# Summing weight blocks in the transfer: four operand sums of a Strassen-type down product move from VectorE to accumulating transfers

## The chip, the cores and the metric

One core of one Trainium2 chip. The time is that of one execution on the device in microseconds (us). The kernel before takes 1230.37 us (median of 3 runs, 1229.37 to 1232.88); its profiled execution took 1231.72 us, of which the trace spans 1229.9. Engines: PE is TensorE, PEld its weight loads, DVE is VectorE, ACT is ScalarE, POOL is GpSimd, SP is SyncE, which issues all transfers of the kernel before. Lnnn is a line of the kernel; most additions, subtractions and products of two tiles stand under one helper's line (L894 `tt`, L138 `sub`), so tiles tell them apart.

## The reference, cut to what matters

One layer of a decoder on 1024 tokens of width 1024, float32. Its last part is the gated MLP:

```python
h = rmsnorm(x, ffn_pre_norm)
u = causal_depthwise_conv(h @ w_up, conv_w, conv_b)     # 1024 x 5632
gate, up = split(u, 2)
y = (gelu(gate) * up) @ w_down                          # 1024 x 2816 @ 2816 x 1024
x = x + rmsnorm(y, ffn_post_norm)                       # y * rsqrt(mean(y*y) + eps) * g
```

The change touches `@ w_down`, the norm and the sum behind it, that is, the last 235 us.

## The kernel before, in words

**The down product.** Tokens, the 2816 inner rows and the 1024 output columns are each halved, and the product of the two 2x2 block matrices is formed from seven block products instead of eight (the Winograd form of Strassen's method). They run in the order P1, P2, P7, P5, P6, P3, P4 (`PASS`). Each is 512 tokens by 1408 by 512: 11 *pairs* `p` (ND = 11) of 128 inner rows, and in each pair four token tiles of 128 (`down`). Operands are split into a rounded part and a rest (`split`: ACT casts, L923; DVE subtracts, L138), and three matmuls of 512 columns (L141 to L143, `mm3`) replace one. A pair is so 12 matmuls, a product 132.

**Weights.** P1, P2 and P3 use a block of the weights as it is: w1 and w2 are the upper and lower 1408 rows, LO and HI the halves of the columns. Four products need sums of blocks:

```
P7: w2[HI] - w1[HI]           P5: w1[HI] - w1[LO], stored to td[0]
P6: w2[HI] - td[0], stored to td[1]        P4: w2[LO] - td[1]
```

`w_load` brings both terms into one 128x1024 tile `dwr` by SP's queue, `t_sum` subtracts on DVE (L894 `dwr<-dwr`), SP stores what a later product needs. `td` lies in DRAM. The tiles have a tag of their own with six buffers (PB), so a load waits until the tile six before it is done with.

**Activations.** The left operands `dg` are loaded from DRAM once; `s_sum` builds S1 to S4 in place on DVE (L894 `dg<-dg`).

**Results.** `evac` takes each product's four PSUM tiles to the SBUF tiles `y`, `combine` adds the products up, `norm1` takes the squares (ACT, L119, into `junk`, sums in `dsq`) and multiplies `y` by the norm's gains `gff` in place (DVE); it so waits for ACT to have read `y`. `norm2` adds up the two sums of squares (L1256), forms mean + eps (L111), takes the power -1/2 on POOL (L112) and does y * r + x on DVE (L1260, two halves), and SP stores the rows.

**The tail.** The last three pairs (TAIL) of P4 are not run pair by pair but token tile by token tile: all three pairs of tile 4, then of tile 5, 6 and 7, so that tile 4 can go through `evac`, `norm1` and `norm2` while PE works on tile 5.

**What sets the order.** Each step is put in a list with a time in units of one pair (`at_`; `t0` is the pair's own time, `tf_` the same with the last pairs moved together). The list is sorted and issued in this order, and ACT, DVE, POOL and PE keep it (`manual_schedule`). The times only order; they make nothing wait. SP's transfers are not in it: a scheduler puts them in order by when it thinks them ready, and SP issues them strictly one after another, each when its own waits are over.

Of the kernel before, what the change touches and what calls it, by code (L numbers as in the profile page):

```python
# [9 lines left out]
F32 = mybir.dt.float32  # L10
# [49 lines left out]
def trunk_kernel(ctx: ExitStack, tc: tile.TileContext, a: dict, out: bass.AP):  # L60
# [832 lines left out]
    def tt(eng, out_, x, y, op):  # L893
        eng.tensor_tensor(out=out_, in0=x, in1=y, op=op)  # L894
# [262 lines left out]
                "P6": lambda: g1[p][:, LO], "P3": lambda: g2[p][:, LO], "P4": lambda: g2[p][:, HI]}[m]()  # L1157

    def b_of(m, p):
        return wr[m, p][:, HI if m == "P5" else LO]  # L1160

    def w_load(m, p):
        early = m == "P1"
        t = wr[m, p] = S("dwr", tag="s" if early else "p", bufs=None if early else PB)
        w1, w2 = a["w_down"][p], a["w_down"][ND + p]
        src = {"P1": ((LO, w1[:, LO]),), "P2": ((LO, w2[:, LO]),), "P7": ((LO, w1[:, HI]), (HI, w2[:, HI])),
               "P5": ((slice(0, 1024), w1),), "P6": ((LO, w2[:, HI]), (HI, td[0, p])), "P3": ((LO, w2[:, HI]),),
               "P4": ((LO, w2[:, LO]), (HI, td[1, p]))}[m]
        for sl, x in src:
            load(t[:, sl], x)  # L1170

    def t_sum(m, p):
        t = wr[m, p]
        if m == "P7":
            tt(V, t[:, LO], t[:, HI], t[:, LO], ALU.subtract)
        elif m == "P5":
            tt(V, t[:, HI], t[:, HI], t[:, LO], ALU.subtract)
            load(td[0, p], t[:, HI])
        else:
            tt(V, t[:, LO], t[:, LO], t[:, HI], ALU.subtract)  # L1180
            if m == "P6":
                load(td[1, p], t[:, LO])

    def s_sum(m, p):
        a1, a2 = g1[p], g2.get(p)
# [10 lines left out]
    def form(m, p, side):  # L1196
        forms[m, p, side] = split(b_of(m, p) if side else a_of(m, p))
        if side:
            del wr[m, p]
        elif m == "P4":  # L1200
            del g2[p]

# [43 lines left out]
    def norm1(t, c):  # L1246
        if t not in sqs:
            sqs[t] = cst.tile([P, 2], F32, name=f"dsq{t}")
        hs = blk(c, 512)
        square_sum(sqs[t][:, c:c + 1], y[t][:, hs])  # L1250
        tt(V, y[t][:, hs], y[t][:, hs], env2["g"][:, hs], ALU.mult)

    def norm2(t):
        xt = env2.pop(("x", t))
        s_, r = sm("zs", 1), sm("zr", 1)
        V.tensor_reduce(out=s_, in_=sqs[t], axis=AX.X, op=ALU.add)  # L1256
        rstd(r, s_, D)
        for c in range(2):
            hs = blk(c, 512)
            V.scalar_tensor_tensor(out=y[t][:, hs], in0=y[t][:, hs], scalar=r, in1=xt[:, hs], op0=ALU.mult, op1=ALU.add)  # L1260
            if t == NT - 1:
                load(out[0, blk(t), hs], y[t][:, hs])
        if t < NT - 1:
            load(out[0, blk(t), :], y[t])

    def x_get(t):
        env2["x", t] = S("x2r", tag="pt", bufs=2) if t < 2 else S("x2r")
        load(env2["x", t], x2d[blk(t), :])

    TAIL = 3  # L1270
    down_items = []

    def at_(tm, f, *x):
# [142 lines left out]
```

## Time and profile before

| | |
|---|---|
| median of 3 runs | 1230.37 us |
| profiled execution, and its span | 1231.72 us, 1229.9 us |
| PE, DVE, ACT, POOL busy in the span | 94%, 75%, 47%, 23% |
| chain of work that ended last | PE 72%, DVE 13%, DMA 6%, issue 3% |
| down product: first and last matmul | 995.4 us, 1214.38 us |
| last matmul to the end of the span | 15.5 us |

The shares are means over stages of quite different kinds; the down product and its norm are the stage from 995.4 us to the end. The seven products begin at 995.4, 1025.35, 1055.27, 1085.19, 1115.11, 1146.53 and 1176.70 us. Four of them take 29.92 us to a hundredth or three, which is 132 matmuls without a gap, 0.2267 us each, and 2.72 us for a pair. That makes the unit of the time list 2.72 us.

### The profile page before, as it was taken

Reading aid. Unit: us, or ns where it says so; the run is one execution under the profiler, and the core shown is the slowest. Engines: PE = TensorE matmul, PEld = TensorE weight load, DVE = VectorE, ACT = ScalarE, POOL = GpSimd, SP = SyncE. Lnnn points to the kernel's source line nnn. Section 1 sums busy time; section 2 is a strip of 40 time slices with the busy share of each in tenths; the row PEclk is TensorE's granted clock in tenths of the full one; section 3 lists DMA queues with packets and bytes.
Section 4 is the critical chain, followed back from the end, with each engine's and each line's share of the span. In section 5 each row is a group of like instructions: output and inputs, shape, how many; then the busy total and the mean of one; then the engine's idle time right before and its main releaser. Section 6 shows DMA issues by size and latency. Waiting matters only on the chain.

```text
span 1229.9 us, 15584 instructions
## 1 busy us (share of the span) xinstructions
PE 1154.8 (94%) x5634; PEld 957.8 (78%) x5634; DVE 917.1 (75%) x1393; ACT 581.5 (47%) x1175; POOL 284.3 (23%) x186
## 2 busy tenths in 40 slices
PE   7987989899987899999999999999999999999993
PEld 6965877678875688877888888888888888887872
DVE  6225664745568988864578998898898988896996
ACT  6313552224356677754554544443444455354441
POOL 1132231315259445450001122122121210000000
PEclk9997998889998999999999999999999999999997
DMA  9373222612293123123022221221212289577673
GB/s 344 117 238 104 70 59 79 224 35 69 70 252 73 35 69 87 54 92 113 18 86 94 79 103 69 86 94 61 103 69 86 103 314 353 161 224 232 196 240 137
DMA packets 68461, 156.47 MB, mean 127 GB/s; under 512 B 7168, under 2 KB 23088, under 8 KB 68384
## 3 DMA queue, kind: packets, MB, share of 16 engines
q1 hardware_dynamic: 68384, 155.48, 38.2%
q8 instruction: 44, 0.72, 0.2%
q14 instruction: 33, 0.27, 0.1%
HBM read 116.78 MB, written 37.63 MB: 126 GB/s over the span
## 4 chain that ended last, share of the span: by engine, by line
PE 72%; DVE 13%; DMA 6%; issue 3%; ACT 3%; POOL 1%; SPq 1%; DVEq 0%; POOLq 0%; ACTq 0%
PE p L141 6%; PE p L143 6%; PE p L142 6%; PE scd L608 3%; PE xz L141 3%; PE xz L142 3%; DVE wf L138 3%; PE xz L143 3%; PE psct L141 2%; PE psct L143 2%; PE psct L142 2%; PE accd L641 2%; PE pso L143 2%; PE pso L141 2%; PE pso L142 2%
## 5 line engine op out<-in xcount | busy, mean ns | idle before, releaser
L871 DVE SCALAR_TENSOR_TENSOR u<-C,cw,u 128x1023 f32<-128x1023 f32 (+1 forms) x88 | 112.3, 1278 | 11.5 <-ACT u L868 11.4
L894 POOL TENSOR_TENSOR sq<-sq,sq 128x512 f32<-128x512 f32 x18 | 29.5, 1638 | 354.2 <-DVE sq L894 354.2
L868 ACT ACTIVATE u<-C,cw 128x1024 f32<-128x1024 f32 x44 | 54.8, 1245 | 113.4 <-DVE C L894 88.3
L923 ACT CAST wf<-dwr 128x512 fp32r<-128x512 f32 x77 | 48.0, 623 | 83.1 <-DVE dwr L894 66.1
L141 PE MATMUL p<-h2h,wf 128*128 128x512 f32 x216 | 84.0, 389 | 0.0
L142 PE MATMUL p<-h2l,wf 128*128 128x512 f32 x216 | 84.0, 389 | 0.0
L143 PE MATMUL p<-h2h,wf 128*128 128x512 f32 x216 | 84.0, 389 | 0.0
L138 POOL TENSOR_TENSOR wl<-wraw,wh 128x1024 fp32r<-128x1024 f32 (+1 forms) x25 | 54.5, 2181 | 109.8 <-DVE wh L132 52.7
L112 POOL TENSOR_TENSOR zr<-var,mhalf 128x1 f32<-128x1 f32 x24 | 13.2, 549 | 262.2 <-DVE var L111 262.2
L141 PE MATMUL psct<-hTh,wh 128*128 128x512 f32 x176 | 71.4, 406 | 1.9 <-DVE oBC L588 1.5
L641 PE MATMUL accd<-pt,v 128*128 128x256 f32 (+1 forms) x336 | 60.5, 300 | 11.7 <-ACT pt L134 5.3
L134 ACT CAST pt<-tpd 128x512 fp32r<-128x512 f32 (+1 forms) x80 | 42.1, 543 | 60.2 <-PE tpd L631 48.4
L142 PE MATMUL psct<-hTl,wh 128*128 128x512 f32 x176 | 70.1, 398 | 0.0
L143 PE MATMUL psct<-hTh,wl 128*128 128x512 f32 x176 | 70.0, 397 | 0.0
L618 ACT ACTIVATE pd<-scd,nm 128x128 f32<-128x128 f32 (+3 forms) x64 | 47.5, 744 | 42.9 <-DVE nm L616 28.3
L641 PEld LDWEIGHTS accd<-pt,v 128*128 128x128 f32 x336 | 50.5, 200 | 19.1 <-ACT pt L134 7.9
L138 DVE TENSOR_TENSOR wf<-wraw,wf 128x512 fp32r<-128x512 f32 x90 | 61.5, 683 | 2.7 <-ACT wf L923 2.7
L138 DVE TENSOR_TENSOR pt<-tpd,pt 128x512 fp32r<-128x512 f32 (+1 forms) x80 | 49.5, 632 | 17.5 <-ACT pt L134 17.2
L138 DVE TENSOR_TENSOR wf<-dwr,wf 128x512 fp32r<-128x512 f32 x77 | 52.6, 684 | 12.1 <-ACT wf L923 11.9
L141 PE MATMUL xz<-hTf,wf 128*128 128x512 f32 x144 | 56.0, 389 | 0.0
L143 PE MATMUL p<-hTf,wf 128*128 128x512 f32 x144 | 56.0, 389 | 0.0
L143 PE MATMUL xz<-hTf,wf 128*128 128x512 f32 x144 | 56.0, 389 | 0.0
(291 smaller groups left out, 3561.3 us busy)
## 6 DMA issues: line engine op xcount, KB each, us to landing
wraw<-in_w_up_dram SPq DMA_DIRECT2D x44, 512.0 KB, 4.2
dwr<-in_w_down_dram SPq DMA_DIRECT2D x77, 256.0 KB, 4.9
gd<-u SPq DMA_DIRECT2D x22, 512.0 KB, 2.6
dg<-gd SPq DMA_DIRECT2D x22, 512.0 KB
wraw<-in_wqk_dram SPq DMA_DIRECT2D x11, 512.0 KB, 4.3
dwr<-in_w_down_dram SPq DMA_DIRECT2D x11, 512.0 KB, 5.0
td<-dwr SPq DMA_DIRECT2D x22, 256.0 KB, 5.3
dwr<-td SPq DMA_DIRECT2D x22, 256.0 KB, 4.3
```

Of the source, the lines that this page charges most:

```text
L134: A.copy(dst, src)
L138: (eng or G).tensor_tensor(out=dst, in0=x, in1=hi.bitcast(F32), op=ALU.subtract)
L141: T.matmul(ps, lhsT=lh, rhs=rh, start=start, stop=False)
L142: T.matmul(ps, lhsT=lh, rhs=rl, start=False, stop=False)
L143: T.matmul(ps, lhsT=ll, rhs=rh, start=False, stop=stop)
L608: T.matmul(sc[:, off + c0:off + c1], lhsT=ql[0:rows, blk(i)], rhs=kl[0:rows, c0:c1], start=x == 0, stop=x == len(passes) - 1)
L618: A.activation(p[:, 0:n], s, AF.Exp, bias=nm, accum_out=den[:, i, hd["d"]:hd["d"] + 1])
L641: T.matmul(acc[:, cs], lhsT=hd["v"][:, j], rhs=pt[:, x, bs], start=j == 0 and x == 0, stop=d == 1 and x == 1 and (o == len(ops) - 1 or (o ...
L868: A.activation(us[i], ct2[i], AF.Identity, bias=cw[:, i, 3:4], scale=cw[:, i, 2:3])
L871: V.scalar_tensor_tensor(out=us[i][:, d:], in0=ct2[i][:, 0:SEQ - d], scalar=cw[:, i, 2 - d:3 - d], in1=us[i][:, d:], op0=ALU.mult, op1=ALU ...
L894: eng.tensor_tensor(out=out_, in0=x, in1=y, op=op)
L923: A.copy(f[:, 0], x)
```

## The change

The four sums over weight blocks are made by transfers that add what they read in DRAM to what lies in SBUF (`accum_op=ALU.add`, issued by POOL, `w_add`). The first term is loaded by SP as before and, where it has a minus sign, negated in place on ACT (`w_neg`). The chain of signs is turned so that every second term is added: P7 is -w1[HI] + w2[HI], stored to td[0]; P5 is -w1[LO] + w1[HI], no longer stored; P6 is td[0] + w1[LO]; after P6 has been split it is negated on ACT and stored to td[1] (`w_keep`); P4 is td[1] + w2[LO]. A weight tile now holds two pairs. Loads come 7.6 pairs ahead instead of 4.6, negations 6.0, additions 5.6; the splits stay where they were, at 2.2 and 1.8.

S4 is formed before P6 instead of behind it. The product with the gains goes to a new tile `yg`, and `norm2` is cut in two: `norm_r` (sum, mean, power) and, later in the list, the two halves of y * r + x. TAIL is 4.

```diff
     def b_of(m, p):
-        return wr[m, p][:, HI if m == "P5" else LO]
+        return wr[m, p // 2][:, blk(p % 2, 512)]
 
     def w_load(m, p):
-        early = m == "P1"
-        t = wr[m, p] = S("dwr", tag="s" if early else "p", bufs=None if early else PB)
+        if (m, p // 2) not in wr:
+            early = m == "P1"
+            wr[m, p // 2] = S("dwr", tag="s" if early else "p", bufs=None if early else PB)
         w1, w2 = a["w_down"][p], a["w_down"][ND + p]
...
+        load(b_of(m, p), {"P1": w1[:, LO], "P2": w2[:, LO], "P7": w1[:, HI], "P5": w1[:, LO], "P6": td[0, p],
+                          "P3": w2[:, HI], "P4": td[1, p]}[m])
+
+    def w_neg(m, p):
+        A.mul(b_of(m, p), b_of(m, p), -1.0)
+
+    def w_add(m, p):
+        w1, w2 = a["w_down"][p], a["w_down"][ND + p]
+        G.dma_start(out=b_of(m, p), in_={"P7": w2[:, HI], "P5": w1[:, HI], "P6": w1[:, LO], "P4": w2[:, LO]}[m],
+                    accum_op=ALU.add)
         if m == "P7":
-            tt(V, t[:, LO], t[:, HI], t[:, LO], ALU.subtract)
-        elif m == "P5":
-            tt(V, t[:, HI], t[:, HI], t[:, LO], ALU.subtract)
-            load(td[0, p], t[:, HI])
-        else:
-            tt(V, t[:, LO], t[:, LO], t[:, HI], ALU.subtract)
-            if m == "P6":
-                load(td[1, p], t[:, LO])
+            load(td[0, p], b_of(m, p))
+
+    def w_keep(p):
+        w_neg("P6", p)
+        load(td[1, p], b_of("P6", p))
...
         if side:
-            del wr[m, p]
+            if m == "P6":
+                w_keep(p)
+            if p % 2 or p == ND - 1:
+                del wr[m, p // 2]
...
         square_sum(sqs[t][:, c:c + 1], y[t][:, hs])
-        tt(V, y[t][:, hs], y[t][:, hs], env2["g"][:, hs], ALU.mult)
+        tt(V, y[t, 2][:, hs], y[t][:, hs], env2["g"][:, hs], ALU.mult)
...
-    TAIL = 3
+    TAIL = 4
...
-            at_(tf_ - (5.5 if m == "P1" else 4.6), w_load, m, p)
+            at_(tf_ - (5.5 if m == "P1" else 4.6 if m in ("P2", "P3") else 7.6), w_load, m, p)
+            if m in ("P7", "P5"):
+                at_(tf_ - 6.0, w_neg, m, p)
             if m not in ("P1", "P2", "P3"):
-                at_(tf_ - 2.7, t_sum, m, p)
+                at_(tf_ - 5.6, w_add, m, p)
...
             elif m == "P6":
-                at_(t0 + 5.2, s_sum, "S4", p)
+                at_(t0 - 1.2, s_sum, "S4", p)
...
                 at_(e0 + 0.06, norm1, t + 4, 0)
-                at_(e0 + 0.07, norm2, t + 4)
+                at_(e0 + 0.3, norm_r, t + 4)
+                at_(e0 + 0.6 if t == 3 else e0 + 1.12, norm2, t + 4)
...
-        at_(e6 + 2.2 + 1.6 * t, norm2, t)
+        at_(e6 + 2.2 + 1.6 * t, norm_r, t)
+        at_(e6 + 2.9 + 1.6 * t, norm2, t)
```

**DVE at the end of P4.** `dt` and `dm` are the PSUM tiles of P4, `gff` the gains, `x2r` the residual rows. Before, token tiles 4 and 5:

```order
L894 TENSOR_TENSOR y_9623<-dt_10432,y_9623 128x512
L894 TENSOR_TENSOR y_9623<-y_9623,gff_9889 128x512
L1256 TENSOR_REDUCE zs_10687<-dsq4_10256 128x1
L111 TENSOR_SCALAR var_10690<-zs_10687 128x1
L1260 SCALAR_TENSOR_TENSOR y_9623<-y_9623,zr_10688,x2r_10563 128x512 x2
L894 TENSOR_TENSOR y_9633<-dm_10440,y_9633 128x512
L894 TENSOR_TENSOR y_9633<-y_9633,gff_9889 128x512
```

The same place of the changed kernel:

```order
L894 TENSOR_TENSOR y_9628<-dt_10424,y_9628 128x512
L894 TENSOR_TENSOR yg_10246<-y_9628,gff_9883 128x512
L1260 TENSOR_REDUCE zs_10652<-dsq4_10245 128x1
L111 TENSOR_SCALAR var_10655<-zs_10652 128x1
L894 TENSOR_TENSOR y_9636<-dm_10434,y_9636 128x512
L894 TENSOR_TENSOR yg_10297<-y_9636,gff_9883 128x512
L1268 SCALAR_TENSOR_TENSOR yg_10246<-yg_10246,dr4_10653,x2r_10537 128x512 x2
L1260 TENSOR_REDUCE zs_10679<-dsq5_10296 128x1
```

The evacuation and the gains of tile 5 now stand between the mean of tile 4 and the two instructions that need tile 4's power from POOL.

**ACT while P7 runs.** Casts of P7's operands (`dg` activations, `dwr` weights). Before:

```order
L923 CAST wf_9442<-dwr_9376 128x512
L923 CAST wf_9459<-dg_8858 128x512
L923 CAST wf_9465<-dwr_9403 128x512
L923 CAST wf_9482<-dg_8886 128x512
L923 CAST wf_9488<-dwr_9426 128x512
```

In the changed kernel, for pairs 5 to 8 of P7; `dwr_9455` and `dwr_9501` are P5's tiles for pairs 0, 1 and 2, 3:

```order
L923 CAST wf_9464<-dg_8855 128x512
L1171 ACTIVATE dwr_9431<-dwr_9431 128x512
L923 CAST wf_9471<-dwr_9329 128x512
L923 CAST wf_9487<-dg_8883 128x512
L1171 ACTIVATE dwr_9455<-dwr_9455 128x512
L923 CAST wf_9494<-dwr_9329 128x512
L923 CAST wf_9510<-dg_8905 128x512
L1171 ACTIVATE dwr_9455<-dwr_9455 128x512
L923 CAST wf_9517<-dwr_9380 128x512
L923 CAST wf_9532<-dg_8927 128x512
L1171 ACTIVATE dwr_9501<-dwr_9501 128x512
```

A negation of a later pair's weights now stands between the two casts of each pair.

**SP around the start of P5's loads.** `td` is the sum's place in DRAM. Before, P5's tiles `dwr_9607` to `dwr_9709` hold one pair each:

```order
L97 DMA dwr_9607<-in_w_down_dram 128x1024
L97 DMA dwr_9635<-in_w_down_dram 128x1024
L97 DMA td_5934<-dwr_9518 128x512
L97 DMA td_5934<-dwr_9540 128x512
L97 DMA dwr_9663<-in_w_down_dram 128x1024
L97 DMA dwr_9686<-in_w_down_dram 128x1024
L97 DMA td_5934<-dwr_9562 128x512
```

Now, where `dwr_9280` to `dwr_9431` are P7's tiles from pair 4 on, and `dwr_9455` to `dwr_9546` P5's:

```order
L97 DMA td_5934<-dwr_9280 128x512
L97 DMA dwr_9455<-in_w_down_dram 128x512 x2
L97 DMA td_5934<-dwr_9280 128x512
L97 DMA td_5934<-dwr_9329 128x512 x2
L97 DMA td_5934<-dwr_9380 128x512 x2
L97 DMA dwr_9501<-in_w_down_dram 128x512 x2
L97 DMA td_5934<-dwr_9431 128x512
L97 DMA dwr_9546<-in_w_down_dram 128x512 x2
```

A store of a sum now stands ahead of loads for P5, and it waits for the accumulating transfer that makes the sum. On POOL the 44 accumulating transfers follow the last addition of the up stage with nothing between them, and the eight powers stand behind all of them.

## Rows read from the trace of the kernel before

**Rows 1.** windows, by product: us; busy PE, PEld, DVE, ACT, POOL; clock, DMA share, GB/s

```profile
995.40:1025.35 29.95, 29.89 (x133) 24.39 (x131) 23.53 (x34) 18.33 (x30) 0.00 (x0) 1.00 0.96 362
...
1055.27:1085.19 29.92, 29.92 (x134) 24.78 (x132) 27.43 (x47) 13.23 (x24) 0.00 (x0) 1.00 0.64 198
1085.19:1115.11 29.92, 29.92 (x134) 24.78 (x132) 25.02 (x43) 13.79 (x26) 0.00 (x0) 1.00 0.67 216
1115.11:1146.53 31.42, 30.21 (x133) 24.70 (x132) 24.06 (x40) 15.75 (x32) 0.00 (x0) 1.00 0.71 228
1146.53:1176.70 30.17, 30.17 (x133) 24.70 (x132) 28.69 (x48) 14.54 (x30) 0.00 (x0) 1.00 0.64 201
1176.70:1214.38 37.68, 32.40 (x133) 25.34 (x131) 32.16 (x61) 13.95 (x30) 2.74 (x5) 0.95 0.63 214
1214.38:1229.90 15.52, 0.00 (x0) 0.00 (x0) 8.12 (x17) 1.45 (x4) 1.64 (x3) 0.64 0.30 119
```

**Rows 2.** timeline of PE: start, us, instruction, idle before it and releaser

```profile
1127.59 0.50 PE L142 MATMUL dt<-wf 128*128 128x512 f32 x1 [1.21 <-DVE wf L138]
...
1195.18 0.50 PE L142 MATMUL dt<-wf 128*128 128x512 f32 x1 [1.74 <-DVE wf L138]
...
1203.60 0.50 PE L142 MATMUL dt<-wf 128*128 128x512 f32 x1 [2.69 <-DVE wf L138]
...
1205.41 0.80 PE L142 MATMUL dt<-wf 128*128 128x512 f32 x1 [0.84 <-DVE wf L138]
...
1208.51 0.40 PE L143 MATMUL dm<-wf 128*128 128x512 f32 x1
```

**Rows 3.** window of the slow matmuls among them, same columns as Rows 1

```profile
1200.00:1203.60 3.60, 0.91 (x5) 0.41 (x4) 3.60 (x7) 1.24 (x2) 0.00 (x0) 1.00 0.62 207
...
1205.40:1208.10 2.70, 2.69 (x6) 2.16 (x7) 1.94 (x5) 0.00 (x0) 0.55 (x1) 0.50 0.22 88
```

**Rows 4.** timeline of the last token tile, all engines

```profile
1217.33 0.68 DVE L894 TENSOR_TENSOR y<-dt,y 128x512 f32<-128x512 f32 x1
...
1221.87 0.68 DVE L894 TENSOR_TENSOR y<-dm,y 128x512 f32<-128x512 f32 x1
1222.64 0.63 ACT L119 ACTIVATE junk<-y 128x512 bf16<-128x512 f32 x1 [3.81 <-DVE y L894]
...
1223.40 0.69 DVE L894 TENSOR_TENSOR y<-y,gff 128x512 f32<-128x512 f32 x1 [0.85 <-ACT junk L119]
1224.01 0.15 DVE L1256 TENSOR_REDUCE zs<-dsq 128x1 f32<-128x2 f32 x1
...
1224.49 0.55 POOL L112 TENSOR_TENSOR zr<-var,mhalf 128x1 f32<-128x1 f32 x1 [3.98 <-DVE var L111]
1225.07 1.41 DVE L1260 SCALAR_TENSOR_TENSOR y<-y,zr,x2r 128x512 f32<-128x512 f32 x2 [0.73 <-POOL zr L112]
```

**Rows 5.** waits of DVE in the last six products: us in total, times, longest

```profile
DVE y L894 <- DMA gff<-in_post_dram: 6.8, 1, 6.8
DVE y L1260 <- POOL zr L112: 5.7, 8, 0.7
DVE y L894 <- ACT junk L119: 3.4, 4, 0.9
```

**Rows 6.** groups of instructions, page part 5 and its longer form: count, busy us, mean ns

```profile
L894 POOL TENSOR_TENSOR sq<-sq,sq 128x512 f32<-128x512 f32 x18 | 29.5, 1638 | 354.2 <-DVE sq L894 354.2
...
L923 ACT CAST wf<-dwr 128x512 fp32r<-128x512 f32 x77 | 48.0, 623 | 83.1 <-DVE dwr L894 66.1
...
L894 DVE TENSOR_TENSOR dwr<-dwr 128x512 f32<-128x512 f32 x44 | 30.0, 683 | 2.5 <-DMA dwr<-td 2.5
```

**Rows 7.** waits of ACT in the same stretch

```profile
ACT wf L923 <- DVE dwr L894: 58.5, 34, 8.1
```

**Rows 8.** tile dwr: landing of its transfers, issue to last byte

```profile
DMA to landing us min/median/max: 3.2/4.9/9.3
```

**Rows 9.** waits of the SP queue in 1027 to 1225 us

```profile
SPq L97 <- DMA td<-dwr: 51.4, 18, 5.5
```

More of the change, by code (lines that the diff above doesn't have):

```diff
@@ L1159, in b_of @@
     def b_of(m, p):
-        return wr[m, p][:, HI if m == "P5" else LO]
+        return wr[m, p // 2][:, blk(p % 2, 512)]
     def w_load(m, p):
-        early = m == "P1"
-        t = wr[m, p] = S("dwr", tag="s" if early else "p", bufs=None if early else PB)
+        if (m, p // 2) not in wr:
+            early = m == "P1"
+            wr[m, p // 2] = S("dwr", tag="s" if early else "p", bufs=None if early else PB)
         w1, w2 = a["w_down"][p], a["w_down"][ND + p]
[L1166 to L1173, printed above, removed]
-        if m == "P7":
-            tt(V, t[:, LO], t[:, HI], t[:, LO], ALU.subtract)
-        elif m == "P5":
-            tt(V, t[:, HI], t[:, HI], t[:, LO], ALU.subtract)
-            load(td[0, p], t[:, HI])
-        else:
-            tt(V, t[:, LO], t[:, LO], t[:, HI], ALU.subtract)
-            if m == "P6":
-                load(td[1, p], t[:, LO])
+        load(b_of(m, p), {"P1": w1[:, LO], "P2": w2[:, LO], "P7": w1[:, HI], "P5": w1[:, LO], "P6": td[0, p],
[6 more added lines that the diff above has]
+                    accum_op=ALU.add)
+        if m == "P7":
+            load(td[0, p], b_of(m, p))
+    def w_keep(p):
+        w_neg("P6", p)
+        load(td[1, p], b_of("P6", p))
     def s_sum(m, p):
@@ L1249, in norm1, with norm_r, norm2 @@
         hs = blk(c, 512)
+        if (t, 2) not in y:
+            y[t, 2] = S("yg")
         square_sum(sqs[t][:, c:c + 1], y[t][:, hs])
-        tt(V, y[t][:, hs], y[t][:, hs], env2["g"][:, hs], ALU.mult)
-    def norm2(t):
-        xt = env2.pop(("x", t))
-        s_, r = sm("zs", 1), sm("zr", 1)
+        tt(V, y[t, 2][:, hs], y[t][:, hs], env2["g"][:, hs], ALU.mult)
+    def norm_r(t):
+        s_, r = sm("zs", 1), cst.tile([P, 1], F32, name=f"dr{t}")
         V.tensor_reduce(out=s_, in_=sqs[t], axis=AX.X, op=ALU.add)
         rstd(r, s_, D)
+        sqs[t] = r
+    def norm2(t):
+        xt, yg = env2.pop(("x", t)), y.pop((t, 2))
         for c in range(2):
             hs = blk(c, 512)
-            V.scalar_tensor_tensor(out=y[t][:, hs], in0=y[t][:, hs], scalar=r, in1=xt[:, hs], op0=ALU.mult, op1=ALU.add)
+            V.scalar_tensor_tensor(out=yg[:, hs], in0=yg[:, hs], scalar=sqs[t], in1=xt[:, hs], op0=ALU.mult, op1=ALU.add)
             if t == NT - 1:
-                load(out[0, blk(t), hs], y[t][:, hs])
+                load(out[0, blk(t), hs], yg[:, hs])
         if t < NT - 1:
-            load(out[0, blk(t), :], y[t])
+            load(out[0, blk(t), :], yg)
     def x_get(t):
```

## The prediction, made before the change was run

> **What bounds the kernel now.** I read the windows by product first [rows 1]. PE is busy for all of P7 and P5, where 132 matmuls fill 29.92 us, so these can only become faster by fewer matmuls, which the change doesn't touch. DVE is next, with 24 to 29 us of 30. So anything taken off DVE pays only where PE waits for DVE, and behind the last matmul.
>
> The second view is the timeline of PE, for those waits [rows 2]. There are four of any size: 1.21 us in P6, and 1.74, 2.69 and 0.84 us in P4, each for a split (L138) on DVE. Behind the last two PE runs slowly: 3.10 us from 1205.41 to 1208.51, seven matmuls that take 7 x 0.2267 = 1.59 us at full rate. The granted clock there is 0.50, 1.2 of 2.4 GHz, after a stretch in which PE was busy 0.91 of 3.60 us [rows 3]. P6 is 1.50 us over 29.92, P3 0.25, P4 7.76 (5.27 of waits, 1.51 of clock, 1 of slow restarts). Together 9.5 us: this is all that PE can give back.
>
> The third view is the timeline of the end [rows 4]. Token tiles 6 and 7 begin their evacuations at 1217.33 and 1221.87, 4.54 us apart, long after the last matmul ended at 1214.38. DVE does them in a strict chain: evacuate, wait 0.85 us for ACT's squares since the gains go in place, multiply, mean, wait 0.73 us for POOL's power, two halves of y * r + x. The waits table has the same two lines for all eight tiles and one more: 6.8 us for the gains' load `gff`, which holds DVE just ahead of PE's 1.21 us [rows 5]. PE needs 3 x 3 x 0.2267 = 2.04 us for a tile of the tail, DVE 4.54: DVE sets the end, 15.52 us after the last matmul.
>
> **The change, part by part.**
>
> *Sums on DVE.* 44 subtractions go [rows 6]. One takes 0.683 us alone and 0.61 us from start to start when the next follows at once (1223.40 to 1224.01 in [rows 4]): 44 x 0.61 = 26.8 us of DVE, 6.7 us a product. In P7 and P5 this is idle time won, since PE didn't wait. In P6 and P4 it stands ahead of the splits that PE waited for. ACT's longest wait, 58.5 us for `dwr` sums, goes too [rows 7].
>
> *Negations on ACT.* 22 in P7 and P5, 11 in P6, each like a cast of the same tile, 0.62 us [rows 6]: 6.8 us a product, on 13.2 to 15.8 of 30 us. Hidden by ACT's idle time as long as none waits for its load; that case is a rival.
>
> *S4 earlier.* The same 11 x 0.61 us of DVE, moved out of P3 (28.69 of 30.17 us busy) into P6 (24.06, less 6.7 for its sums) [rows 1]. Cost nothing, covered by that.
>
> *Accumulating transfers.* No row shows one. Loads issued earlier and the td stores are the same bytes as before; only their place changes. In the list an addition is issued 5.6 pairs ahead and its cast stands at 1.8: 3.8 x 2.72 = 10.3 us, and another 1.8 x 2.72 = 4.9 us until PE, of which cast and split take 1.3. From below it is as good as a plain transfer of the block, which lands in 3.2 us at best and 4.9 us in the median; from above I take two plain ones in series at their worst, 2 x 9.3 = 18.6 us [rows 8]. The row nearest in kind, 256 KB with SBUF as an end, is the median, and twice that, 9.8 us, still fits 10.3. I take 5 to 10 us and no stall, and keep 18.6 for the range. POOL has nothing else to do here until P4 [rows 1]; an issue may cost it up to 2.72 us a pair.
>
> What the queues have to carry: P7, P5 and P6 move 198, 216 and 228 GB/s over their windows, 19.5 MB, at shares 0.64, 0.67 and 0.71, which makes 61.5 us of all 16 engines, 318 GB/s when busy. The 33 accumulating transfers there are 8.65 MB of it, 27.2 us for one plain pass. If each counts once, the engines are busy 61.5 of 89.8 us. P1 shows 0.96 at 362 GB/s with PE not held up.
>
> The Trainium skill, "Collectives: The Full Stack", section Part 3, says a reducing transfer is half as fast as a copying one since its add needs two source reads. By that the accumulating transfers count twice and the engines are busy 88.7 of 89.8 us: full, but not over, and the sum below stands; no run here shows it yet.
>
> *The norm.* Out of place the gains no longer wait for the squares (4 x 0.85 us), and with `norm_r` apart, the next tile's evacuation and gains lie in the 0.73 us of waiting for POOL. DVE's work for a tile of the tail is then 2 x 0.61 + 0.35 + 1.41 = 2.98 us instead of 4.54 (0.35 is DVE's part of the 0.48 us from tile 7's mean to POOL's start). PE needs 4 x 3 x 0.2267 = 2.72 us for a tile with four pairs.
>
> *The sum.* Without PE's waits from P7 on, P4 begins at 1055.27 + 4 x 29.92 = 1174.95, tile 4 is done 8 x 2.72 later at 1196.7, and the last matmul ends at 1204.87. What is late next is DVE. Between P3's end and the evacuation of tile 4 its order holds 25 additions, splits and products (15.3 us), four means (1.4 us) and four pairs of y * r + x (5.6 us), with one wait for POOL (0.7 us): 23.0 us, so 1198.1; with 0.9 us for small waits, 1199.0, 2.3 us after PE. From there it needs 8.0 us until the evacuation of tile 7 begins (two tiles ahead, 2.98 us each, and 2.1 us for the first, which waits for its squares): 1207.0. Then evacuation, gains and tile 6's halves (2.63 us), and from tile 7's mean on what [rows 4] show, 1229.90 - 1224.01 = 5.89 us: 1215.5, against 1229.9 now, so -14.4 us. If DVE were not late, PE would set the end at 1213.7. The profiled execution took 1231.72 us, so it becomes 1217.3; the median of the runs is 1.35 us lower, 1216.0. I add 1.5 us, for of four waits in the old P6 and P4 one or another will stay: the splits of the last four pairs are still bunched, and `gff` stands behind a store that waits for ACT. **Forecast 1217.5 us**, its own range 1213 to 1223.
>
> **The rivals.**
>
> *A. The transfers are the bound, slower than before.* If an accumulating transfer takes the engines n times as long as a plain one, P7 to P6 need 61.5 + (n - 1) x 27.2 us of 89.8. Loads are issued 7.6 pairs, 20.7 us, ahead, and the chain of load, negation, addition and split takes 4.9 + 0.6 + 4.9 + 1.3 = 11.7, so 9 us can be made up from run-ahead. PE stalls from n = 2.4; at n = 2.85 the 13 us won are used up, and from there the kernel is slower. At n = 3 it is 115.9 - 89.8 - 9 = 17 us late: 1234.5, and 1245 at most. For it: shares of 0.64 to 0.71 already, and blocks whose rows are half as long as those that ran at 362 GB/s. Against it: P3 follows with one plain load a pair.
>
> *B. Queue order turns latency into waits; faster by little.* SP loads P5's pairs 2 and 3 only after the stores of P7's pairs 8 and 9, which wait for their additions (25.4 in the list). ACT's negation of that load stands ahead of the casts of P7's pair 9, which PE needs at 31. That leaves 5.6 x 2.72 = 15.2 us for addition, load (4.9), negation, cast and split (1.9): 8.4 us for the addition. At 9.8 us each of the three such joints (P7 to P5, P5 to P6, P6's stores ahead of P3's loads) costs 1.4 us, at 18.6 us the first costs 10. I put it at 8 us: 1225.5. SP already waits 51.4 us for td stores to land, 18 times [rows 9]; against it, PE didn't stall there.
>
> *C. The issue is starved.* POOL would get to write a transfer's descriptors only where DVE leaves it room. In P7 DVE is idle 29.92 - 27.43 + 6.7 = 9.2 us after the change. If an issue takes like POOL's other work on a 128x512 tile, 1.64 us [rows 6], 11 need 18.0 us, 8.8 more a product; four products, less 9 us of run-ahead, cost 26 us: 1243.5. The trace shows neither for nor against: POOL issues nothing in it. The page "SBUF — State Buffer", section SBUF: two separate sides, of the Trainium skill describes such a lock-out, for two-port modes of DVE; by that page C applies only if DVE's work here is of that kind, and a 512-column float32 addition at 0.61 us [rows 4] doesn't look like a doubled rate.
>
> **How the numbers follow.** A difference within 0.3%, 3.7 us, can't be told from none. Forecast 0.61, all of it faster. B 0.14 (1221 to 1231): 0.08 faster, 0.06 same. A 0.19: 0.02 faster, 0.05 same, 0.12 slower. C 0.06, slower. Sum: faster 0.71, same 0.11, slower 0.18. The range takes in the forecast's, B and A's half up to n = 3: 1213 to 1235. Nothing in the sum leads below PE's own end, 1213.7 or 1214.2 as a median; the last microsecond is for the scatter of the runs shown.
>
> **What would show it.** Right: no PE wait above 0.5 us in P7 to P3, the clock at 1.00 until the last matmul, evacuations of tiles 4 to 7 about 3 us apart, 10 to 13 us from the last matmul to the end, `dwr` additions landing in 5 to 10 us. A would show as DMA shares of 1 in P7 to P6 and PE waiting for splits whose casts waited for transfers; B as ACT waiting in a negation for a load while PE waits, with shares well under 1; C as POOL's issues further apart than 2.72 us while their waits were over. Wrong altogether: P7 to P6 over 95 us, or evacuations still 4.5 us apart.

## The result, and the profile after

The changed kernel takes 1215.27 us (median of 4 runs, 1214.53 to 1217.49), against 1229.88 us for the kernel before on the same chip: a ratio of 0.988, with a 95% interval of 0.986 to 0.990. The forecast was 1217.5 us. The profiled execution took 1217.49 us and its span is 1215.7.

The windows by product come first, as in [rows 1]: length, busy PE, PEld, DVE, ACT and POOL with their counts, clock, DMA share, GB/s. The products are P1, P2, P7, P5, P6, P3 and P4, each from its first matmul to that of the next, then what lies behind the last matmul.

```profile
997.12:1027.40 30.28, 30.21 (x134) 24.70 (x133) 23.96 (x34) 18.21 (x30) 0.00 (x0) 1.00 0.96 362
1027.40:1057.32 29.92, 29.92 (x134) 24.77 (x133) 21.90 (x36) 22.64 (x42) 9.48 (x11) 1.00 1.07 320
1057.32:1087.23 29.91, 29.91 (x133) 24.77 (x132) 20.68 (x36) 13.29 (x25) 6.44 (x8) 1.00 0.94 259
1087.23:1117.15 29.92, 29.92 (x133) 24.77 (x132) 19.99 (x33) 16.58 (x31) 13.20 (x15) 1.00 0.96 221
1117.15:1147.08 29.93, 29.93 (x134) 24.78 (x133) 23.19 (x38) 22.64 (x46) 0.00 (x0) 1.00 0.65 196
1147.08:1176.99 29.91, 29.91 (x133) 24.77 (x132) 25.28 (x43) 14.27 (x30) 9.74 (x11) 1.00 0.92 216
1176.99:1207.08 30.09, 30.09 (x133) 24.59 (x131) 27.35 (x54) 11.76 (x28) 4.47 (x6) 1.00 0.51 176
1207.10:1215.70 8.60, 0.00 (x0) 0.00 (x0) 4.69 (x11) 0.72 (x2) 1.10 (x2) 0.71 0.46 183
```

The first seven rows have PE busy from end to end at a clock of 1.00; the waits of [rows 2] and the slow clock of [rows 3] are gone, and the waits table of PE is empty for this stretch. P6, P3 and P4 take 29.93, 29.91 and 30.09 us instead of 31.42, 30.17 and 37.68. DVE in P7 fell from 27.43 to 20.68. The next thing to see is the DMA share: 0.94 in P7 and 0.96 in P5 where [rows 1] have 0.64 and 0.67; P6 has 0.65. It is 1.07 already in P2, since the first additions run ahead into it. Before, P2 was:

```profile
1025.35:1055.27 29.92, 29.92 (x134) 24.78 (x132) 23.53 (x39) 13.40 (x25) 0.00 (x0) 1.00 0.72 253
```

In P5 a share of 0.96 moves 221 GB/s where 0.67 moved 216: a byte costs more engine time than before.

The timeline of DVE at the end shows the evacuations (start, us, instruction, idle before it):

```profile
1197.72 1.42 DVE L1268 SCALAR_TENSOR_TENSOR yg<-yg,dr,x2r 128x512 f32<-128x512 f32 x2 [0.66 <-POOL dr L112]
1199.05 0.68 DVE L894 TENSOR_TENSOR y<-dt,y 128x512 f32<-128x512 f32 x1
...
1201.67 0.69 DVE L894 TENSOR_TENSOR y<-dm,y 128x512 f32<-128x512 f32 x1 [0.75 <-PE dm L143]
...
1204.59 0.68 DVE L894 TENSOR_TENSOR y<-dt,y 128x512 f32<-128x512 f32 x1
```

They are 2.62 and 2.92 us apart, and the one after them begins at 1207.49 (the next fence), 2.90 later. In [rows 4] the last two were 4.54 apart. From the last matmul on, all engines:

```profile
1206.69 0.39 PE L143 MATMUL dm<-wf 128*128 128x512 f32 x1
...
1207.49 0.68 DVE L894 TENSOR_TENSOR y<-dm,y 128x512 f32<-128x512 f32 x1
...
1208.21 0.69 DVE L894 TENSOR_TENSOR yg<-y,gff 128x512 f32<-128x512 f32 x1
1208.27 0.63 ACT L119 ACTIVATE junk<-y 128x512 bf16<-128x512 f32 x1 [2.18 <-DVE y L894]
...
1208.82 1.41 DVE L1268 SCALAR_TENSOR_TENSOR yg<-yg,dr,x2r 128x512 f32<-128x512 f32 x2
1210.14 0.14 DVE L1260 TENSOR_REDUCE zs<-dsq 128x1 f32<-128x2 f32 x1
...
1210.56 0.55 POOL L112 TENSOR_TENSOR dr<-var,mhalf 128x1 f32<-128x1 f32 x1 [2.35 <-DVE var L111]
1211.14 1.41 DVE L1268 SCALAR_TENSOR_TENSOR yg<-yg,dr,x2r 128x512 f32<-128x512 f32 x2 [0.66 <-POOL dr L112]
```

The last matmul ends at 1207.08 and the span 8.62 us later; it was 15.52. The square sum on ACT (1208.27) and the gains on DVE (1208.21) now run beside each other, and the 0.85 us of [rows 4] is gone. The last y * r + x still waits 0.66 us for POOL.

Last, the two DMA queues on the page (packets, MB, share of 16 engines over the span), the group of the new transfers, and from the tile's view their issues (ns, min/median/max) and the landing of all `dwr` transfers:

```profile
q1 hardware_dynamic: 63632, 143.95, 35.3%
q0 software_dynamic: 6336, 11.54, 5.4%
...
L1175 POOL DMA_DIRECT2D dwr<-in_w_down_dram x44 | 38.9, 1010 | 138.7 <-ACT dwr L1171 67.5
```

```profile
L1175 POOL DMA_DIRECT2D dwr<-in_w_down_dram x44: 872/874/2284, 1036.8 to 1173.2; - x44
...
DMA to landing us min/median/max: 2.6/7.6/12.3
```

The median landing was 4.9 us in [rows 8]. By the profile's list of transfers the 44 additions alone land in 7.6 us in the median, the plain `dwr` loads of SP in 6.9 instead of 4.9, and the `td` stores in 10.3 instead of 5.3. The issue of a new transfer has its median at 874 ns.

Since the part ahead of the down product is the same in all kernels here, but for how P1's weights are loaded, and yet ends anywhere between 989.9 and 997.1 us in their profiled executions, I compare spans of the trace from the first matmul of the down product on. Before, it begins at 995.05 (the 995.4 us given ahead of the prediction is 0.35 us too late), the last matmul ends 219.33 us later and the span 234.85 later. After, it begins at 997.12, and the two are 209.96 and 218.58. Spans are printed to a tenth of a microsecond, so differences of 0.1 us between them mean nothing. So PE gave back 9.4 us and the part behind it 6.9: 16.3 us together. The span shrank by only 14.2, as this execution began the product 2.1 us later.

### The profile page after: what moved, and what is told of

The parts are those of the page before. It is cut to its first block, busy times and chain, and to the rows that moved or that the text cites. A ratio compares the mean times of both kernels' runs of the same rounds, so it can differ in the third digit from the quotient of the medians.

```text
span 1215.7 us, 15618 instructions
## 1 busy us (share of the span) xinstructions
PE 1154.6 (95%) x5634; PEld 959.4 (79%) x5634; DVE 892.0 (73%) x1349; ACT 597.3 (49%) x1208; POOL 325.1 (27%) x230
## 3 DMA queue, kind: packets, MB, share of 16 engines
q0 software_dynamic: 6336, 11.54, 5.4%
## 4 chain that ended last, share of the span: by engine, by line
PE 69%; DVE 6%; DMA 2%; ACT 2%; issue 2%; POOL 0%; SPq 0%; DVEq 0%; POOLq 0%; ACTq 0%
PE p L141 6%; PE p L142 6%; PE p L143 6%; PE xz L141 3%; PE xz L142 3%; PE xz L143 3%; PE dx L143 2%; PE dx L142 2%; PE dx L141 2%; PE pso L141 2%; PE pso L143 2%; PE pso L142 2%; PE scd L608 2%; PE psct L141 2%; PE psct L142 2%
## 5 line engine op out<-in xcount | busy, mean ns | idle before, releaser
L1175 POOL DMA_DIRECT2D dwr<-in_w_down_dram x44 | 38.9, 1010 | 138.7 <-ACT dwr L1171 67.5
L138 DVE TENSOR_TENSOR wf<-dg,wf 128x512 fp32r<-128x512 f32 x77 | 53.8, 699 | 11.5 <-ACT wf L923 11.3
L141 PE MATMUL xz<-hTf,wf 128*128 128x512 f32 x144 | 56.0, 389 | 0.0
L142 PE MATMUL xz<-hTf,wf 128*128 128x512 f32 x144 | 56.0, 389 | 0.0
L143 PE MATMUL xz<-hTf,wf 128*128 128x512 f32 x144 | 56.0, 389 | 0.0
## 6 DMA issues: line engine op xcount, KB each, us to landing
td<-dwr SPq DMA_DIRECT2D x22, 256.0 KB, 10.3
```

Of the source, the lines that this page charges most:

```text
L138: (eng or G).tensor_tensor(out=dst, in0=x, in1=hi.bitcast(F32), op=ALU.subtract)
L141: T.matmul(ps, lhsT=lh, rhs=rh, start=start, stop=False)
L142: T.matmul(ps, lhsT=lh, rhs=rl, start=False, stop=False)
L143: T.matmul(ps, lhsT=ll, rhs=rh, start=False, stop=stop)
L1175: G.dma_start(out=b_of(m, p), in_={"P7": w2[:, HI], "P5": w1[:, HI], "P6": w1[:, LO], "P4": w2[:, LO]}[m], accum_op=ALU.add)
```

## The experiments

My theory was that the gain has two halves that hardly depend on each other: the sums leave DVE, so PE stops waiting, and the norm leaves its strict chain, so the end gets shorter; the transfers and POOL pay for it with time that nothing waits for. Rivals: one edit alone does it; the transfers are close to being the bound; the issue order alone hides their latency.

**One half each.** The first kernel has the sums alone, with the old norm, old S4 and three pairs by row tile. The second has the norm and the four pairs alone, with the sums on DVE. Against the changed kernel and the kernel before:

```diff
 # sums alone, against the changed kernel
-        tt(V, y[t, 2][:, hs], y[t][:, hs], env2["g"][:, hs], ALU.mult)
+        tt(V, y[t][:, hs], y[t][:, hs], env2["g"][:, hs], ALU.mult)
...
-    TAIL = 4
+    TAIL = 3
...
-                at_(t0 - 1.2, s_sum, "S4", p)
+                at_(t0 + 5.2, s_sum, "S4", p)
 # norm and tail alone, against the kernel before
+    def norm_r(t):
...
-    TAIL = 3
+    TAIL = 4
```

> The accumulating transfers alone: S4, the norm and TAIL = 3 are those of the kernel before. Theory (two separate gains: the sums taken off DVE give PE's waits back, the norm's order gives the end back): no PE wait above 0.5 us from P7 to the last matmul, but tiles 4 to 7 still evacuate 4.5 us apart, so the last evacuation begins about 37.6 us after P4's start (23.8 us for tile 4 + 0.2 + 3 x 4.54) and the end is 8.0 us later: 45.6 us after P4's start, against 38.5 in the changed kernel, so about 1222. Rival (PE's waits in P4 came from the norm's own waits on DVE, not from the sums): PE still waits about 5 us in P4, 1227 to 1230.

> The norm out of place, its split into two steps and TAIL = 4 alone; sums on DVE and S4 as before. Theory: DVE still carries 11 sums of 0.61 us in P4, PE still waits there and in P6 (4 us or more in all), but the end comes 8 to 9 us after the last matmul instead of 15.5: 1221 to 1224. Rival (the norm's waits were the cause of PE's waits): PE's waits in P4 go as well, 1217 or less.

Sums alone: 1220.86 us, ratio 0.993 (0.991 to 0.995). The last matmul ends 210.64 us after the product's first, the span 226.66. Norm and tail alone: 1220.46 us, ratio 0.994 (0.992 to 0.996); 214.44 and 225.26. Against 234.85 these are 8.2 and 9.6 us, 17.8 in sum, and both together, with the early S4 that neither half has, give 16.3. So neither edit alone explains the gain. With sums alone the timeline of DVE keeps the old spacing at the end:

```profile
1204.31 0.68 DVE L894 TENSOR_TENSOR y<-dt,y 128x512 f32<-128x512 f32 x1
1205.84 0.69 DVE L894 TENSOR_TENSOR y<-y,gff 128x512 f32<-128x512 f32 x1 [0.85 <-ACT junk L119]
...
1207.51 1.42 DVE L1263 SCALAR_TENSOR_TENSOR y<-y,zr,x2r 128x512 f32<-128x512 f32 x2 [0.73 <-POOL zr L112]
1208.84 0.68 DVE L894 TENSOR_TENSOR y<-dm,y 128x512 f32<-128x512 f32 x1
```

Evacuations at 1204.31 and 1208.84 are 4.53 us apart. With norm and tail alone, the windows of P6, P3 and P4, the last one up to the last matmul's end, show DVE full in P3 and P4 and PE short of work in P6 and P4:

```profile
1117.22:1149.02 31.80, 30.22 (x133) 24.70 (x132) 24.00 (x40) 16.69 (x34) 0.00 (x0) 1.00 0.69 231
1149.02:1178.94 29.92, 29.92 (x133) 24.77 (x132) 29.82 (x50) 13.89 (x29) 0.00 (x0) 1.00 0.65 209
1178.94:1211.58 32.64, 30.98 (x133) 24.36 (x131) 31.58 (x62) 13.58 (x29) 3.94 (x6) 1.00 0.64 228
```

The three products together take 94.36 us, 4.9 less than the 99.27 of [rows 1]. So the norm, too, removes waits of PE: 4.9 us alone, where the sums alone remove 8.7, and both 9.4. The waits that both halves take are in P4, which falls from 37.68 to 32.64 us by the norm and tail alone; P6 stays long, at 31.80 instead of 31.42, until the sums go. My theory for this half had 4 us or more of waits left, which holds; its end of 8 to 9 us does not.

P6's wait has another cause than a full DVE. Before, and with norm and tail alone, DVE stands idle just ahead of it, waiting for the transfer that brings the gains:

```profile
1126.24 0.69 DVE L894 TENSOR_TENSOR y<-y,gff 128x512 f32<-128x512 f32 x1 [6.76 <-DMA gff<-in_post_dram]
...
1128.72 0.69 DVE L894 TENSOR_TENSOR yg<-y,gff 128x512 f32<-128x512 f32 x1 [7.13 <-DMA gff<-in_post_dram]
```

The first row is the kernel before, the second the norm and tail alone. In the kernel before, SP waits 3.6 us for a `td` store to land and issues `gff` only at 1121.34, 6.2 us into P6. In the changed kernel it goes out at 1109.19, 8.0 us ahead of P6, and no wait for it is left, nor is one with the sums alone. So P6's 1.5 us come back with the order of SP's transfers, which the new sums changed. No run moves that load alone, so this cause is read from the traces and not tested.

Behind the last matmul it is the other way round: the sums alone lose 0.5 us (16.02 instead of 15.52), since the evacuations stay 4.53 us apart; the norm and tail alone bring 4.7 (10.82), both 6.9. DVE begins tile 4's evacuation 4.9 us ahead of the last matmul's end with norm and tail alone and 8.0 us ahead with both.

**The smaller parts.** The changed kernel with three pairs by row tile, with the old norm, and with S4 at its old place:

```diff
 # three pairs
-    TAIL = 4
+    TAIL = 3
 # old norm
-        tt(V, y[t, 2][:, hs], y[t][:, hs], env2["g"][:, hs], ALU.mult)
+        tt(V, y[t][:, hs], y[t][:, hs], env2["g"][:, hs], ALU.mult)
...
-                at_(e0 + 0.3, norm_r, t + 4)
-                at_(e0 + 0.6 if t == 3 else e0 + 1.12, norm2, t + 4)
+                at_(e0 + 0.07, norm2, t + 4)
 # S4
-                at_(t0 - 1.2, s_sum, "S4", p)
+                at_(t0 + 5.2, s_sum, "S4", p)
```

> The changed kernel with TAIL = 3. Theory: PE stays without waits, but a tile takes PE only 2.04 us in the tail and DVE 2.9, so evacuation of tile 7 begins 3 x 2.9 us after that of tile 4 (23.9 us after P4's start), 32.6 us after P4's start instead of 30.3: 1.5 to 2.5 us slower than the changed kernel, 1217 to 1218. Rival (TAIL adds nothing once DVE is free): same as the changed kernel within 0.5 us.

> The changed kernel with the old norm: gains in place, mean, power and the two halves in one step; accumulating transfers, early S4 and TAIL = 4 stay. Theory: PE without waits, tiles 4 to 7 evacuate 4.5 us apart again from 22 us after P4's start, the last at 35.6, the end 8.0 us later: 43.6 us after P4's start against 38.5, so 5 us slower than the changed kernel, about 1220. Rival (the end was DVE's load, not its chain of waits): less than 2 us slower.

> The changed kernel with the S4 sums of half-tensors back at their old place, 5.2 instead of -1.2 from the product's start. My theory: in the changed kernel DVE is busy 25.3 of 29.9 us in P3 and some 20 to 23 in P5 and P6, so moving 6.7 us of sums by one product finds room either way; TensorE shows no wait over 0.5 us, the last matmul ends 210.0 us (within 0.5) after the down product's first matmul, as in the changed kernel, and the end comes 218.6 us (within 1) after it; the time is within 0.3% of the changed kernel's. Rival: the old place fills DVE in the product before the last, its tail work starts late, and either TensorE waits or the end comes 1 to 3 us later.

Times: 1216.18 us (ratio 0.991, 0.988 to 0.994), 1219.38 (0.993, 0.990 to 0.996) and 1214.25 (0.988, 0.984 to 0.992); all three intervals overlap that of the changed kernel. The traces are sharper. From the product's first matmul to the end they take 220.57, 224.60 and 219.64 us instead of 218.58: three pairs cost 2.0 us, the old norm 6.0, the old S4 1.1. With three pairs PE leaves less time between token tiles and the last three evacuations follow 3.14 us apart and wait for no PE: DVE sets them. With the old norm these two waits of DVE are back (total, times, longest):

```profile
DVE y L1263 <- POOL zr L112: 5.7, 8, 0.7
DVE y L894 <- ACT junk L119: 3.4, 4, 0.9
```

They are [rows 5] again, 5.7 and 3.4 us. For S4, my theory said that there is room either way; the rival said that DVE fills. The windows of P6 and P3 with S4 at its old place:

```profile
1112.52:1142.44 29.92, 29.92 (x133) 24.77 (x132) 17.76 (x29) 20.23 (x41) 0.00 (x0) 1.00 0.62 201
1142.44:1172.95 30.51, 30.30 (x133) 24.62 (x132) 30.51 (x52) 16.08 (x34) 7.07 (x8) 1.00 0.77 178
```

DVE works 17.76 us in P6 and 30.51 of 30.51 in P3, and its evacuation of tile 4 comes 203.86 us after the product's first matmul instead of 201.93. The rival was right, at the low end of what it named: TensorE lost 0.6 us and the end came 1.1 later.

**The price of the adding.** The changed kernel with plain transfers in the same places; the second half overwrites the first, so the sums are left out.

```diff
-        G.dma_start(out=b_of(m, p), in_={"P7": w2[:, HI], "P5": w1[:, HI], "P6": w1[:, LO], "P4": w2[:, LO]}[m],
-                    accum_op=ALU.add)
+        G.dma_start(out=b_of(m, p), in_={"P7": w2[:, HI], "P5": w1[:, HI], "P6": w1[:, LO], "P4": w2[:, LO]}[m])
```

> The changed kernel with plain transfers where the accumulating ones were: the second half of the weights overwrites the first, so the sums are left out, and bytes, issues, queue and order stay. It prices the adding alone. My theory: an adding transfer takes about 1.9 times the engine share of a plain one (176 against 335 GB/s in the profile of the changed kernel), so the share of the POOL queue falls from 5.4% to about 2.8%, and the median landing on it from 7.6 us to 4 to 5; the issue on POOL stays at 0.87 us; the time doesn't move (within 0.3%), since nothing waited for the landings. Rival: the POOL queue moves such blocks slowly whether it adds or not: share and landing stay. Second rival: the adding costs TensorE or the loads something that the waits don't show: 2 us or more faster.

The page's line of POOL's queue and the group, and the landing of `dwr`:

```profile
q0 software_dynamic: 3520, 11.54, 2.9%
...
L1175 POOL DMA_DIRECT2D dwr<-in_w_down_dram x44 | 24.2, 551 | 151.8 <-ACT dwr L1171 80.5
```

```profile
L1175 POOL DMA_DIRECT2D dwr<-in_w_down_dram x44: 546/546/768, 1033.7 to 1169.7; - x44
...
DMA to landing us min/median/max: 2.6/5.0/7.8
```

The same 11.54 MB take 2.9% of the engines instead of 5.4%: an adding transfer costs 1.9 times a plain one. The landing falls from 7.6 to 5.0 us for all of `dwr`, loads included; the 44 alone land in 5.1 us, and the `td` stores in 4.9 instead of 10.3, so the adding delayed the transfers beside it too. Against my expectation the issue gets cheaper too: from 0.87 to 0.55 us (medians), with 3520 packets instead of 6336, 80 a transfer instead of 144. And the time is 1213.61 us, ratio 0.987 (0.984 to 0.991); from the product's first matmul to the end it is 218.65 us, the same as the changed kernel's to the tenth that the trace gives. The adding is hidden.

**How near the transfers are to being the bound.** Behind each adding transfer, one or two extra plain copies of 256 KB from DRAM to DRAM go on the same queue; nothing reads them.

```diff
+    tx = dram.tile([2, 7, ND, P, 512], F32, name="tx")
...
                     accum_op=ALU.add)
+        for k in range(2):
+            G.dma_start(out=tx[k, PASS.index(m), p], in_=(w1, w2)[k][:, HI])
```

> The changed kernel with one extra plain copy of a 256 KB block from DRAM to DRAM behind each of the 44 adding transfers, on the same queue; nothing reads the copies. It asks how near the transfers are to being the bound (rival A of the prediction). 11 copies a product at the 335 GB/s of a plain byte are about 8.6 us of engine time more, so a share of some 1.2 to 1.3 where it was 0.94 to 1.07. My theory: the shares near 1 in the products with adding transfers come from work done ahead of need, so there is some room left: TensorE waits little (under 3 us) and the last matmul ends 210 to 214 us after the product's first. Rival: the transfers are already full, every microsecond added is paid for: the last matmul 15 us later or more.

> The same with two extra copies behind each adding transfer: some 17 us of engine time more in a product of 29.9 us, a share of 1.5 or more by sum, over the whole stretch from P7 to P4 (about 150 us) 69 us more. My theory: now the transfers are the bound, additions land too late for the split, TensorE waits in P5, P6 and P4 and its clock may fall: the time is 10 to 40 us longer than the changed kernel's. Rival: the share counts overlapped time and the engines have more room than it says: the last matmul within 3 us of the changed kernel's.

One copy: 1217.61 us, ratio 0.988 (0.985 to 0.992), no wait on PE, the last matmul 210.01 us after the first, and the end 1.8 us later than without. Two copies: 1240.93 us, ratio 1.007 (1.004 to 1.010), last matmul at 234.01. Windows of P2, P7 and the next two stretches of 29.9 us, with one copy:

```profile
1026.00:1055.90 29.90, 29.90 (x134) 24.75 (x133) 21.95 (x37) 19.91 (x38) 11.80 (x16) 1.00 1.05 336
1055.90:1085.80 29.90, 29.90 (x134) 24.75 (x133) 20.62 (x34) 14.37 (x26) 12.89 (x18) 1.00 1.08 313
1085.80:1115.70 29.90, 29.90 (x134) 24.75 (x133) 20.07 (x32) 17.91 (x34) 15.75 (x22) 1.00 1.07 300
1115.70:1145.60 29.90, 29.90 (x134) 24.75 (x133) 22.78 (x37) 22.57 (x47) 7.16 (x10) 1.00 0.94 279
```

With two copies:

```profile
1026.00:1055.90 29.90, 29.90 (x134) 24.76 (x133) 21.86 (x37) 19.46 (x37) 12.37 (x18) 1.00 1.05 355
1055.90:1085.80 29.90, 29.90 (x134) 24.76 (x133) 17.24 (x29) 12.63 (x24) 16.00 (x24) 1.00 1.07 334
1085.80:1115.70 29.90, 26.54 (x102) 18.03 (x101) 16.31 (x26) 14.71 (x27) 16.99 (x27) 1.00 1.08 331
1115.70:1145.60 29.90, 27.19 (x107) 19.16 (x105) 17.62 (x28) 16.46 (x31) 17.05 (x27) 1.00 1.07 329
```

With one, the share already stands at 1.05 to 1.08 in three windows and PE loses nothing: it is back to 0.94 in the fourth, when they are through with their work ahead. With two, it stays at 1.05 to 1.08 through all four, at 329 to 355 GB/s, and PE falls to 26.54 and 27.19 of 29.90. So a share near 1 by itself didn't say that the transfers were the bound: what counts is the sum over all products. My estimate of a share of 1.2 to 1.3 was wrong; no window here goes above 1.08.

Part of both losses comes by way of POOL. Its powers for the norm stand in its order behind the issues of the last additions and copies, and DVE waits for the first of them; here with one copy, then with two:

```profile
1184.23 1.41 DVE L1271 SCALAR_TENSOR_TENSOR yg<-yg,dr,x2r 128x512 f32<-128x512 f32 x2 [2.49 <-POOL dr L112]
...
1209.41 1.41 DVE L1271 SCALAR_TENSOR_TENSOR yg<-yg,dr,x2r 128x512 f32<-128x512 f32 x2 [9.11 <-POOL dr L112]
```

In the changed kernel this wait is 0.46 us. The 2.0 us more account for the end that comes 1.8 us later with one copy. With two, PE's longest wait for a split, 2.98 us, ends right behind DVE's 9.11, and some 5 of the 24 us are lost there, slow matmuls at a granted clock of 0.57 (1212 to 1216 us) included; the others are lost in P5 and P6, where ACT's casts wait 62.5 us for `dwr` transfers (31.6 with one copy, 3.2 without).

**The lead.** The changed kernel with loads, negations and additions drawn together, so that they stand closer to their use:

```diff
-            at_(tf_ - (5.5 if m == "P1" else 4.6 if m in ("P2", "P3") else 7.6), w_load, m, p)
+            at_(tf_ - (5.5 if m == "P1" else 4.6 if m in ("P2", "P3") else 4.6), w_load, m, p)
-                at_(tf_ - 6.0, w_neg, m, p)
+                at_(tf_ - 3.4, w_neg, m, p)
-                at_(tf_ - 5.6, w_add, m, p)
+                at_(tf_ - 3.2, w_add, m, p)
```

> The changed kernel with its list entries drawn together for P7, P5, P6 and P4: load 4.6 instead of 7.6 ahead of use, negation 3.4 instead of 6.0, addition 3.2 instead of 5.6. My theory: the lead is what hides the latency: load about 4.9 us, negation 0.6, addition 7.6 to 10.3 us and the split on ACT and DVE 2 make a chain of 15 us or so, some 5.5 pairs of 2.72 us, more than 4.6; TensorE waits for split weights in these products, and the time is 5 to 25 us longer than the changed kernel's. Rival: the numbers only order the instructions, each engine runs as far ahead as its buffers let it, and the time stays within 2 us of the changed kernel's, with no wait over 0.5 us on TensorE.

It takes 1223.06 us, ratio 0.995 (0.993 to 0.997). The last matmul ends at 216.46 us and the span at 227.52, 6.5 and 8.9 us later than in the changed kernel. The waits of PE and the first one of ACT:

```profile
PE dx L141 <- ACT wf L923: 1.4, 3, 0.5
PE dt L142 <- DVE wf L138: 1.2, 2, 1.0
PE dx L142 <- DVE wf L138: 0.7, 3, 0.2
```

```profile
ACT wf L923 <- DMA dwr<-in_w_down_dram: 46.0, 23, 6.7
```

ACT's casts wait 46.0 us for `dwr` transfers where they wait 3.2 in the changed kernel. The waits shown on PE itself are 3.3 us in sum, those on its weight loads 8.0, and the last matmul is 6.5 us late. So the time in the list matters, as I expected, and the rival (each engine runs as far ahead as its buffers let it) is wrong. It is the latency of rival B of the prediction that PE then pays, and the lead in the list keeps it away.

**The end once more.** The changed kernel with the last mean ahead of the scaling of tile 6:

```diff
-                at_(e0 + 0.6 if t == 3 else e0 + 1.12, norm2, t + 4)
+                at_(e0 + (1.12, 1.12, 1.35, 0.6)[t], norm2, t + 4)
```

> The changed kernel with the reduction of the norm's last tile ahead of the scaling of the tile before it, in DVE's order. In the profile of the changed kernel the last reduction starts 1.32 us after the product of tile 6 on DVE, and the last scaling is released by POOL's reciprocal 0.66 us after DVE was free. My theory: the last reduction starts about 0.6 to 1 us earlier, the last scaling by as much less the scaling of tile 6 that then stands between; the end comes 0.3 to 0.8 us sooner after the last matmul (8.62 us now). Too small for the times. Rival: the reduction only swaps with the scaling, the store of tile 6 goes out later and the end doesn't move, or moves 0.3 us later.

```profile
1204.90 0.68 DVE L894 TENSOR_TENSOR y<-dm,y 128x512 f32<-128x512 f32 x1
...
1206.43 0.15 DVE L1260 TENSOR_REDUCE zs<-dsq 128x1 f32<-128x2 f32 x1
...
1206.70 2.74 DVE L1268 SCALAR_TENSOR_TENSOR yg<-yg,dr,x2r 128x512 f32<-128x512 f32 x4
```

The timeline of DVE shows the last mean at 1206.43, 1.53 us after its evacuation began instead of 2.65, and no wait for POOL: both scalings in a row, four halves, end at 1209.44, 0.5 us sooner. But the store of tile 6 now goes out right ahead of those of tile 7: behind the last scaling 3.7 us pass at 223 GB/s, where the changed kernel has 3.15 us at 166, and the span ends 8.72 us after the last matmul, as against 8.62, no sooner to the tenth that the trace gives. The time, 1213.31 us (ratio 0.987, 0.983 to 0.991), can't be told from the changed kernel's. The rival was right: the end doesn't move. That the stores take what DVE gives is how I read these two windows; no run tests it apart. No version here beats the changed kernel by more than the noise.

## Why the prediction was right, step by step

*PE's waits.* Right in size. The 9.5 us that I took from [rows 2, 3] are 9.4 by the trace. The 1.5 us that I added for waits that would stay were not needed: none stayed. For P6, 1.5 of these 9.5 us, the reason was wrong, though I had the wait for `gff` before me: I put it to the sums on DVE, and said under rival B that PE didn't stall where SP waits for `td` stores. In P6 it did: by the trace SP's wait held back `gff`, `gff` held DVE for 6.8 us, and DVE then held PE. That these 1.5 us came back as counted is luck. And the wait for ACT's squares, which I read for all eight tiles, stands four times in [rows 5]; the sum used four.

*Sums, negations, S4.* Right in kind. S4's cost was called nothing because the sums of P6 leave; with S4 left where it was, DVE fills in P3 and 1.1 us is lost, so moving it is a small gain of its own, which I had not counted.

*Accumulating transfers.* A landing of 5 to 10 us was right (7.6 in the median of the 44), and so was no stall. Their price is 1.9 plain transfers, 5.4% against 2.9% of the span. The Trainium skill, "Collectives: The Full Stack", section Part 3, says that a reducing transfer is half as fast as a copying one, for its two source reads; these runs agree, at 1.9. By that the engines were to be 88.7 of 89.8 us busy from P7 to P6. The windows give 0.94, 0.96 and 0.65 there, 76 us, since work moved ahead into P2 (1.07).

*POOL's issue.* Bounded by 2.72 us; it is 0.87.

*The end.* Here a term was mis-sized. "Between P3's end and the evacuation of tile 4" I took 23.0 us of DVE, and 0.9 for small waits: 23.9. From 1177.05, at P3's end, to 1199.05 it is 22.0 us: 23 instead of 25 additions, splits and products at 0.61 (14.0), four means (1.1), four pairs of y * r + x (5.3), and waits for POOL of 0.46, 0.44 and 0.66. So DVE was about level with PE at tile 4, not 2.3 us late. From there on its evacuations follow each other by 2.6 to 2.9 us and PE needs 2.72 us for a tile; tile 5's waits for PE, and tile 7's begins 0.4 us behind the last matmul. So PE set the end to within 0.4 us: it is my "if DVE were not late" case, 1213.7, which is 218.65 us from the product's first matmul. Measured are 218.58. My sum had 220.45 before the 1.5 were added.

The sign that I named for this, "10 to 13 us from the last matmul to the end", was missed for the same reason: it is 8.6. The forecast for the profiled execution was 1218.8 and it took 1217.49. That these are only 1.3 us apart is in part luck: the 1.9 and the 1.5 us that I had too much were partly made up for by a start of the product 2.1 us later in this execution, which belongs to no part of the change.

*The rivals.* A did not occur, though the shares near 1 in P7 and P5 that I named as its sign did: by its own sum it begins at n = 2.4, and n is 1.9. With one copy behind each, the POOL queue's share is 7.6%, 2.6 times the 2.9% of plain transfers, and still nothing stalls; with two it is 9.8% of a longer span, 3.4 times, and the last matmul is 24 us late. So A was possible, but the stall begins at a higher price than I had put, between these two, and the copies only stand in for it: nothing reads them. B did not occur at the lead chosen, and cost 8.9 us of trace at a shorter one. C did not occur: an issue at 0.87 us (0.55 for a plain one) leaves POOL two thirds of a pair free, with DVE busy 20 to 27 of 30 us; POOL's longest waits were for ACT's negations, 67.5 us, 40.3 of them ahead of the first addition.

## What to carry to other kernels

An addition of two blocks that are both loaded from DRAM can leave the compute engines at about 1.9 times the transfer time of its second operand, if its landing is covered by lead; look up the sum of DMA work over all stages, not the share of one. Where an engine waits for DVE in the middle and the end hangs on DVE too, take DVE's work from both: here either alone gave 8 to 10 us, together 16. What else stands in the order of the engine that issues such transfers waits behind their issues, as the norm's powers on POOL did with the copies. Before moving the last instructions of a chain, see what the stores behind them do.

## What the runs showed of the hardware

- An adding transfer of 256 KB into SBUF takes 144 packets and 0.87 us of issue on POOL; a plain one in its place 80 packets and 0.55 us. It takes 1.9 times the engine time of the plain one, and `td` stores beside it land in 10.3 us instead of 4.9.
- The DMA share of a window went to 1.08 and no higher, with 300 to 355 GB/s moved at shares from 1.05 up.
- The down product's first matmul came anywhere in 989.9 to 997.1 us in the kernels here, with the same code ahead of it but for the loads of P1's weights. That spread of 7.2 us is half the gain, and it hides edits of 1 to 2 us in the times.
